# Merge factors loaded ahead of the next pair's inputs, merges and strided items at other steps, in a hybrid decoder step

## The chip, the cores and the metric

The kernel runs on one core of a Trainium2 chip. The core has five engines with a program of their own each: TensorE (PE in the profile; PEld is its loading of weights), VectorE (DVE), ScalarE (ACT), GpSimd (POOL) and SyncE (SP), which in this kernel issues nearly all DMAs. The metric is the device time of one execution in microseconds (us), as the median of several runs.

## The reference

One layer of a decoder on a prompt of 2048 positions (width 1024) and on 32 sample rows (8 sequences of 4 positions, each with a cache of 2048 keys and values). Everything is float32.

```python
q, k, v, u, vg = split(rmsnorm(x) @ w_in)
outs, lses = [], []
for (w, d), bias in zip(((128, 1), (512, 4), (2048, 16)), biases):   # 8 heads of 64
    o, lse = dilated_attention(q, k, v, bias, d, w // d + 1)
    outs.append(o); lses.append(lse)
weights = softmax(stack(lses), axis=0)
att = sum(weights[..., None] * stack(outs))                            # the merge
gate = spatial_gate(layernorm(vg))
x = x + concat([att, u * gate]) @ w_out
x = x + swiglu(rmsnorm(x))
y = rmsnorm(x)
```

Outputs are y for prompt and samples, and the new windows of keys and values.

## The kernel before

The work has three parts in time: the input projection (with the attention of the sample rows beside it), the attention of the prompt, and the output projection with the feed-forward block. The change concerns the middle part and its two borders.

**Order.** The whole order is written out by hand. A `Plan` (L46) collects calls as (step, phase) and then emits them sorted by step, and within a step by ten phases: early, exp, low, scores, turn, mid, values, out, misc, store. Every engine and SP executes its own instructions in the order in which they were emitted. An instruction that waits holds everything behind it on its engine; for SP this means that a DMA that can't be issued yet holds all later DMAs. A step is a place in this order and no length of time.

**Pairs and items.** The 8 heads are worked in 4 pairs, `p` = 0 to 3. Prompt attention begins at step B0 = 240; a pair has 20 units of two steps, so a stage of NI = 40 steps. L = 399 is the step where the pairs end. Sixteen units of a pair are band items (numbered 0 to 15, 128 queries each; branches 1 and 2 together), four are strided items ("s", the third branch). The lists FIRST, OTHER and LAST (L1137 to L1139) give the order of units for pair 0, for pairs 1 and 2, and for pair 3. A unit with index i of its pair has its scores at step X = stage start + 2i + 1.

- A band item: scores on PE (`pair_scores`, L890 and L897), bias and row minimum on DVE (L903), exponential on ACT (L908), transposes on PE (L919), values on PE (L942, L952), output to `ob` by ACT (L959).
- A strided item: `strided_order` (L967, two copies on POOL at X-4) gathers its keys and queries into `sq`; scores on PE at X (L977); bias and minimum on DVE for each head of the pair (L984, L985, at X+1 and X+2); a subtraction on POOL (L989, at X+2 and X+3); exponential on ACT (L992); row sums on DVE (L996); transposes on PE (L1001, at X+5 and X+6), copied by ACT (L1003); values on PE (L1010); output to `o3` by ACT (L1017).

**Merging.** When a pair is through, `Stats` turns minima and sums into the two merge factors per position and head: a selection on POOL (L1034), a small matmul (L1040), arithmetic on DVE (L1050 to L1066), and a store to `f_d` in DRAM by eight DMAs (L1073), at step 6 of the next pair's stage. `merge_load(p, j)` (L1079, DMAs at L1087) loads the factors for two blocks of 256 positions, j and j+1, spread over the partitions, two DMAs of 256 KB into one "pair" tile of which there are two. `merge` (L1091) needs three POOL instructions for each of the eight blocks: L1096 (`ob` times factor), L1098 (`o3` times factor), L1100 (sum). `merge_store` (L1102) writes the merged rows to `cat_d`, four blocks at a time. All this is planned beside the work of the next pair; only the output projection reads `cat_d`.

For pair 3 the first four blocks are merged before L: blocks 0 and 2 by DVE, 1 and 3 by POOL (L1183). The other four are merged in the output projection.

**Other loads in these stages.** `load_head(p)` (L851) loads the next pair's q and k (1 MB each, L857), bias (L860), values in the strided order (L845) and values in band order (four DMAs with short rows, L849), planned at steps 4, 6, 8, 15 and 18 of the stage before (L1166). `load_far` (L878) loads the values of branch 2's far keys. `sgu_sample_cat_load` (L1110, DMA at L1112) loads the 32 sample rows' attention and gate output from `cs_d` into a "pair" tile at step B0+19; `sgu_sample_cat` (L1114) transposes them on PE at step B0+22 (L1119). They were written to `cs_d` before B0 (L617).

**The border to the output projection.** From step L-12 on, weights of w_out are loaded (`load_wo`, L1354) and split into a high and a low part on ACT and POOL (L142, L145); from L-9 on, `early_cat` (L1393) loads rows of `cat_d`, partly into tiles that hold `ob` and `o3` in the pairs.

Of the kernel before, what the change touches and what calls it, by code (L numbers as in the profile page):

```python
# [10 lines left out]
F32 = mybir.dt.float32  # L11
# [8 lines left out]
P = 128  # L20
T = 2048
NT = T // P
# [19 lines left out]
def dap(t, offset, pattern):  # L42
    return bass.AP(tensor=t.tensor, offset=t.offset + offset, ap=pattern)


class Plan:  # L46
# [8 lines left out]
    def at(self, step, phase, fn, *args):  # L55
        self.events.append((step, self.PHASES.index(phase), self.n, fn, args))
        self.n += 1
# [10 lines left out]
def hymba_step(ctx: ExitStack, tc: tile.TileContext, A: dict, O: dict):  # L68
    nc = tc.nc
    sync, act, dve, pool, pe = nc.sync, nc.scalar, nc.vector, nc.gpsimd, nc.tensor  # L70
# [97 lines left out]
    at = plan.at  # L168
# [4 lines left out]
    def zn_tile():  # L173
        return rp.tile([P, 512], F32, name="zn", tag="zn", bufs=3)

    def pair_tile(dtype=F32R):
        return rp.tile([P, 2, 512], dtype, name="pair", tag="pair", bufs=2)
# [4 lines left out]
    def raw_tile():  # L182
        return rp.tile([P, 512], F32, name="raw", tag="raw", bufs=RAW)
# [475 lines left out]
    B0 = 240  # L659
# [22 lines left out]
    for j in range(8):  # L682
        s0 = 105 + 4 * j if j < 3 else 117 + 3 * (j - 3) if j < 6 else 127 + 3 * (j - 6)
# [27 lines left out]
    for half in range(2):  # L711
        for ki, kind in enumerate(ORDER[half]):
            for gi, tiles in enumerate(GROUPS):
# [13 lines left out]
                for j, tj in enumerate(tiles):  # L727
# [24 lines left out]
                    else:  # L752
                        layer_norm(e + 1, t, lambda t=t: zn["g", t], P, lambda t=t: gate_tile(t))

                        f = e + 4 + ((3 if half else 5) if tj in (4, 5) else 0)
# [19 lines left out]
    for n in range(MADE):  # L775
        s0 = 138 + 15 * n
# [11 lines left out]
    for run in key_runs:  # L788
        for j, (b, t, u) in enumerate(run):
            s0 = 36 + i if i < 8 * EARLY else 60 + int((i - 8 * EARLY) * 4 / 3)  # L790
# [12 lines left out]
    for bg in range(2):  # L803
        s0 = (136, V0 + 24)[bg]
# [4 lines left out]
    for b in range(SB):  # L809
        s0 = V0 + 8 * b  # L810
# [266 lines left out]
    mf = {}  # L1077

    def merge_load(p, j):  # L1079

        if p < HP - 1:
            f = pair_tile(F32)
            t_ = f[:, 0], f[:, 1]
        else:
            t_ = raw_tile(), zn_tile()
        for c in range(2):
            sync.dma_start(t_[c], dap(f_d, (p * 8 + j + c) * 2 * CP * 512, [[512, 2 * CP], [0, C // CP], [1, 512]]))  # L1087
            v = t_[c].rearrange("p (i z r) -> p i z r", z=2, r=NT)
            mf[p, j + c] = v[:, :, 0], v[:, :, 1]
# [45 lines left out]
        (strided_scores if its[0]["kind"] == "s" else pair_scores)(*its)  # L1135

    FIRST = [0, 1, 2, 3, "s", 4, 5, "s", 6, 7, 8, "s", 9, 10, 11, "s", 12, 13, 14, 15]  # L1137
    OTHER = [0, "s", 1, 2, 3, 4, "s", 5, 6, 7, 8, "s", 9, 10, 11, 12, "s", 13, 14, 15]
    LAST = ["s", 0, 1, "s", 2, 3, "s", 4, 5, "s", 6, 7] + list(range(8, NT))  # L1139
    units, taken = [], set()  # L1140
    for p in range(HP):
        r4 = 0
        for n in FIRST if p == 0 else LAST if p == HP - 1 else OTHER:
            X = B0 + 2 * len(units) + 1
# [7 lines left out]
            if n % 2:  # L1152
                grp["y"] = (4, 5, 6) if p == HP - 1 and n == NT - 1 else (6, 6, 7)
                taken.update(range(X + grp["y"][0], X + grp["y"][2]))
    NI = 2 * len(OTHER)
    L = B0 + 2 * len(units) - 1
# [6 lines left out]
    for p in range(1, HP):  # L1163
        s0 = B0 + (p - 1) * NI
        at(s0 + 4, "misc", begin, p)
        for y in (4, 6, 8, 15, 18):  # L1166
            at(s0 + y, "misc", load, p)

    def stats_of(p, steps, r0, r1):
        d = {}  # L1170
        at(*steps[0], lambda: d.update(s=Stats(p, sts[p], r0, r1, dve if r0 else pool)))
        for (y, ph), fn in zip(steps, "a b c weights_e weights_b store".split()):
            at(y, ph, lambda fn=fn: getattr(d["s"], fn)())

    for p in range(HP):
        s0 = B0 + (p + 1) * NI
        if p == HP - 1:
            x = s0 - NI
            stats_of(p, [(x + y, ph) for y, ph in ((26, "early"), (27, "turn"), (28, "early"), (28, "early"), (29, "early"), (29, "mid"))], 0, 64)
            steps = ((2, "early"), (2, "turn"), (3, "early"), (4, "early"), (5, "early"), (5, "early"))  # L1180
            for j in (0, 2):
                at(x + 30, "mid", merge_load, p, j)
            for j, y, eng in ((0, 33, dve), (1, 33, pool), (2, 36, dve), (3, 36, pool)):  # L1183
                for part in range(3):
                    at(x + y + part, "store", merge, p, j, eng, part)
            at(x + 36, "store", merge_store, p, 0, 2)
            at(x + 39, "store", merge_store, p, 2, 4)
        else:
            steps = ((2, "misc"), (3, "misc"), (4, "early"), (5, "early"), (5, "misc"), (6, "mid"))
            fast = p == HP - 2  # L1190
            y0 = 12
            when = [y0 + (i * 2 // 3 if fast else i) for i in range(24)]
            for j in range(0, 8, 2):
                at(s0 + max(8, when[3 * j] - 4) + (j == 2), "mid", merge_load, p, j)
            for i, y in enumerate(when):
                at(s0 + y, "store", merge, p, i // 3, pool, i % 3)
            for j in (0, 4):
                at(s0 + when[3 * j + 11] + 1, "store", merge_store, p, j, j + 4)
        stats_of(p, [(s0 + y, ph) for y, ph in steps], 64 if p == HP - 1 else 0, P)
    for X, its in units:  # L1200
        p, n = its[0]["p"], its[0]["n"]
# [21 lines left out]
        if n % 2:  # L1223
            y = its[0]["grp"]["y"]
# [9 lines left out]
    for n in range(3):  # L1234
        at(B0 + 40 + 30 * n, "store", down_plain, n)

    at(B0 + 19, "misc", sgu_sample_cat_load)
    at(B0 + 22, "scores", sgu_sample_cat)

    plan.run(B0)  # L1240
# [4 lines left out]
    ap_ = left.enter_context(tc.tile_pool(name="attn", bufs=2, reuse_waits="tile"))  # L1245
# [929 lines left out]
    def first_block(B):  # L2175
# [5 lines left out]
        load_cat(B, 0, KD - 1, KD)  # L2181
        load_cat(B, 5, 0, KD)
        merge_load(h, 4)
        merge_load(h, 6)
        load_acc(B, 1)
# [325 lines left out]
```

## Time and profile before

| | us |
|---|---|
| median of 3 runs | 2467.8 (2467.05 to 2472.98) |
| profiled execution, its own time | 2461.96 |
| its span, first to last instruction | 2460.2 |
| PE busy | 2350.1 |
| POOL busy | 1438.1 |
| stretch of pair 0 / 1 / 2 / 3 | 68.7 / 74.2 / 73.5 / 77.9 |
| from the end of the pairs to the end | 1604.4 |

The times of steps below come from the profiled execution, which was 5.8 us faster than the median run. In the profile L12 is line 12 of the kernel, "out<-in" are the names of tiles, and "x4" counts instructions of a kind that were merged into one row. SPq is SP's queue: its durations are the time that SP needed to issue a DMA, not the time of the transfer. A bracket `[6.53 <-ACT e L992]` gives the time for which the engine stood idle before the instruction, and the instruction that released it.

### The profile page before, as it was taken

The numbers are of one execution on the slowest core, as the hardware profiler recorded it, in microseconds if no ns is written. First come the engines' busy times: TensorE is split into PE (matmuls) and PEld (weight loads), VectorE is DVE, ScalarE is ACT, GpSimd is POOL, SyncE is SP. The second block draws the span as 40 slices with busy tenths as digits, with TensorE's granted clock in tenths as the row PEclk, the third lists the DMA queues.
The fourth block names the chain that finished last, engine by engine and source line by source line (L and its number), as shares of the span: only waits on it lengthen the run. The fifth ranks groups of instructions, "written<-read, shape, count | busy, mean of one in ns | idle before, by whom it ended". The sixth has DMA issues, their size and how long they took to land. (4 is left out here: it accounts for less than half of the span.)

```text
span 2460.2 us, 41718 instructions
## 1 busy us (share of the span) xinstructions
PE 2350.1 (96%) x14592; PEld 2026.5 (82%) x14592; DVE 1482.7 (60%) x2902; ACT 1203.3 (49%) x2745; POOL 1438.1 (58%) x1153
## 2 busy tenths in 40 slices
PE   8999999997988899999999999999999998999998
PEld 6877786665666678999999988999999977999997
DVE  3467573114555534767777676566666666677676
ACT  6424333224555546656665546444443446555555
POOL 2225463112345646888788764756666563888885
PEclk9999999998989898999999999999999998999999
DMA  9864856786554564887877654766666644878552
GB/s 276 248 193 138 247 160 212 226 255 172 143 149 119 153 199 137 256 265 229 256 243 232 209 164 152 262 205 215 200 214 216 212 125 164 271 244 249 172 171 88
DMA packets 333365, 494.61 MB, mean 201 GB/s; under 512 B 42903, under 2 KB 174176, under 8 KB 329572
## 3 DMA queue, kind: packets, MB, share of 16 engines
q1 hardware_dynamic: 326308, 479.90, 63.4%
q10 hardware_dynamic: 6848, 12.06, 1.8%
q8 instruction: 115, 1.88, 0.3%
q14 instruction: 94, 0.77, 0.1%
HBM read 404.72 MB, written 168.98 MB: 233 GB/s over the span
## 5 line engine op out<-in xcount | busy, mean ns | idle before, releaser
L1626 POOL TENSOR_TENSOR op<-fr,op 128x512 fp32r<-128x512 f32 x392 | 522.5, 1342 | 350.6 <-ACT op L1622 262.1
L1863 PE MATMUL ps_m<-xh,op 128*128 128x384 f32 (+3 forms) x1344 | 429.9, 320 | 3.9 <-DVE raw L1874 3.5
L1864 PE MATMUL ps_m<-xl,op 128*128 128x384 f32 (+3 forms) x1344 | 428.6, 319 | 1.6 <-POOL xl L145 1.5
L1865 PE MATMUL ps_m<-xh,op 128*128 128x384 f32 (+3 forms) x1344 | 429.0, 319 | 0.0
L1716 DVE TENSOR_TENSOR acc<-acc,ps_o 128x512 f32<-128x512 f32 x448 | 300.3, 684 | 71.1 <-PE ps_o L1714 63.8
L1714 PE MATMUL ps_o<-hop 128*128 128x512 f32 x1142 | 322.6, 394 | 1.7 <-DVE hop L1695 1.0
L1863 PEld LDWEIGHTS ps_m<-xh,op 128*128 128x128 f32 x1344 | 256.7, 191 | 13.2 <-DVE raw L1874 6.7
L1864 PEld LDWEIGHTS ps_m<-xl,op 128*128 128x128 f32 x1344 | 256.4, 191 | 7.3 <-POOL xl L145 2.0
L1865 PEld LDWEIGHTS ps_m<-xh,op 128*128 128x128 f32 x1344 | 256.3, 191 | 0.0
L1714 PEld LDWEIGHTS ps_o<-hop 128*128 128x128 f32 x1142 | 209.4, 188 | 37.7 <-DVE hop L1695 2.8
L1622 ACT ACTIVATE op<-fr 128x512 fp32r<-128x512 f32 x396 | 239.3, 621 | 0.0
L325 PE MATMUL ps_s<-wh,xh 128*128 128x512 f32 x480 | 197.1, 411 | 6.1 <-ACT xh L142 6.0
L326 PE MATMUL ps_s<-wl,xh 128*128 128x512 f32 x480 | 190.0, 396 | 0.0
L327 PE MATMUL ps_s<-wh,xl 128*128 128x512 f32 x480 | 189.7, 395 | 0.0
L1863 PE MATMUL ps_t<-xh,op 128*128 128x384 f32 (+2 forms) x560 | 180.7, 323 | 5.5 <-ACT xh L1512 2.5
L1864 PE MATMUL ps_t<-xl,op 128*128 128x384 f32 (+2 forms) x560 | 179.9, 321 | 0.5 <-DVE xl L1534 0.3
L1865 PE MATMUL ps_t<-xh,op 128*128 128x384 f32 (+2 forms) x560 | 179.9, 321 | 0.0
L546 POOL TENSOR_TENSOR pr<-kv,qb 96x512 f32<-96x512 f32 x32 | 46.5, 1452 | 158.1 <-DMA kv<-in_cache_k_dram 77.0
L1695 POOL TENSOR_TENSOR hop<-hop 128x512 fp32r<-128x512 f32 x96 | 130.9, 1364 | 11.9 <-ACT hop L1691 11.4
L325 PEld LDWEIGHTS ps_s<-wh,xh 128*128 128x128 f32 x480 | 91.6, 191 | 41.4 <-issue 16.8
L1714 PE MATMUL ps_m<-hop 128*128 128x512 f32 x384 | 119.5, 392 | 0.0
L1877 ACT ACTIVATE zn<-zn 128x384 f32<-128x384 f32 (+2 forms) x65 | 31.6, 487 | 171.5 <-DVE zn L1876 171.5
(568 smaller groups left out, 5391.3 us busy)
## 6 DMA issues: line engine op xcount, KB each, us to landing
fr<-ab_d SPq DMA_DIRECT2D x308, 256.0 KB
hop<-dd_d SPq DMA_DIRECT2D x143, 256.0 KB
out_ks_dram<-in_cache_k_dram SPq DMA_DIRECT2D x56, 512.0 KB
out_vs_dram<-in_cache_v_dram SPq DMA_DIRECT2D x56, 512.0 KB
ab_d<-fr SPq DMA_DIRECT2D x88, 256.0 KB
dwx<-dd_d SPq DMA_DIRECT2D x71, 256.0 KB
ab_d<-pair SPq DMA_DIRECT2D x63, 256.0 KB
kv<-in_cache_k_dram SPq DMA_DIRECT2D x64, 192.0 KB
```

Of the source, the lines that this page charges most:

```text
L325: pe.matmul(o[j], xh[:, k, :], wh, start=(k == 0), stop=False)
L326: pe.matmul(o[j], xh[:, k, :], wl, start=False, stop=False)
L327: pe.matmul(o[j], xl[:, k, :], wh, start=False, stop=(k == KD - 1))
L546: eng.tensor_mul(pr[0:n], x[0:n], q[0:n])
L1622: act.activation(ops[f, j][0], ab[f][j], AF.Copy)
L1626: (pool if f > 1 or j in POOL_LOW[f] or B.b0 else dve).tensor_sub(lo_, ab[f][j], hi.bitcast(F32))
L1695: (pool if B.b0 or k >= 7 * (NF // 2 - 1) else dve).tensor_sub(lo_, lo_.bitcast(F32), hi.bitcast(F32))
L1714: pe.matmul(ps, l_, r_, start=(new and y == 0), stop=(y == 2), skip_group_check=True)
L1716: dve.tensor_add(x[:, cs], x[:, cs], ps)
L1863: pe.matmul(out, wh[:, ks], xh[:, :, k], start=(k == 0 and q not in (2, 4, 6)), stop=False, skip_group_check=True)
L1864: pe.matmul(out, wh[:, ks], xl[:, :, k], start=False, stop=False, skip_group_check=True)
L1865: pe.matmul(out, wl[:, ks], xh[:, :, k], start=False, stop=(k == 3), skip_group_check=True)
```

## The change

With s0 the start of the stage in which a pair's merge is done:

- `merge_load` takes its tiles for j = 4 and 6 from two new buffers "mf" (4 KB per partition each); for j = 0 and 2 it uses the two "pair" tiles as before.
- The four calls of `merge_load` stand at s0+7 to s0+10. They stood at s0+8, 15, 20 and 26 (for the merge of pair 2: 8, 13, 16 and 20).
- Merges begin at s0+15 (for the merge of pair 2 at s0+14); they began at s0+12. Their stores move with them.
- q, k and bias of pairs 2 and 3 are loaded at steps 11, 12 and 13 of the stage before, not at 4, 6 and 8. Pair 1's are left.
- In OTHER the four strided items have places 3, 8, 12 and 16 of 20 instead of 1, 6, 11 and 16; in LAST 2, 4, 7 and 9 instead of 0, 3, 6 and 9.
- In pair 3, block 2 is merged by POOL instead of DVE, blocks 2 and 3 at other steps, and each has a store of its own.
- The sample rows are loaded at B0+2 instead of B0+19.

```diff
     def merge_load(p, j):
         if p < HP - 1:
-            f = pair_tile(F32)
+            f = pair_tile(F32) if j < 4 else ap_.tile([P, 2, 512], F32, name="mf", tag="mf", bufs=2)
...
-    OTHER = [0, "s", 1, 2, 3, 4, "s", 5, 6, 7, 8, "s", 9, 10, 11, 12, "s", 13, 14, 15]
-    LAST = ["s", 0, 1, "s", 2, 3, "s", 4, 5, "s", 6, 7] + list(range(8, NT))
+    OTHER = [0, 1, 2, "s", 3, 4, 5, 6, "s", 7, 8, 9, "s", 10, 11, 12, "s", 13, 14, 15]
+    LAST = [0, 1, "s", 2, "s", 3, 4, "s", 5, "s", 6, 7] + list(range(8, NT))
...
         at(s0 + 4, "misc", begin, p)
-        for y in (4, 6, 8, 15, 18):
+        for y in (11, 12, 13, 15, 18) if p > 1 else (4, 6, 8, 15, 18):
             at(s0 + y, "misc", load, p)
...
-            for j, y, eng in ((0, 33, dve), (1, 33, pool), (2, 36, dve), (3, 36, pool)):
+            for j, y, eng in ((0, 33, dve), (1, 33, pool), (2, 35, pool), (3, 38, pool)):
                 for part in range(3):
                     at(x + y + part, "store", merge, p, j, eng, part)
             at(x + 36, "store", merge_store, p, 0, 2)
-            at(x + 39, "store", merge_store, p, 2, 4)
+            at(x + 39, "store", merge_store, p, 2, 3)
+            at(x + 42, "store", merge_store, p, 3, 4)
...
-            y0 = 12
+            y0 = 14 if fast else 15
             when = [y0 + (i * 2 // 3 if fast else i) for i in range(24)]
             for j in range(0, 8, 2):
-                at(s0 + max(8, when[3 * j] - 4) + (j == 2), "mid", merge_load, p, j)
+                at(s0 + 7 + j // 2, "mid", merge_load, p, j)
...
-    at(B0 + 19, "misc", sgu_sample_cat_load)
+    at(B0 + 2, "misc", sgu_sample_cat_load)
```

## The prediction

> **What bounds the kernel now.** I read the page first, for the engine that sets the span.
>
> ```profile
> PE 2350.1 (96%) x14592; PEld 2026.5 (82%) x14592; DVE 1482.7 (60%) x2902; ACT 1203.3 (49%) x2745; POOL 1438.1 (58%) x1153
> ```
>
> PE is the bound on the whole, so time is won only where PE stands still or runs at a low clock. The busy times by stretch say where. I cut at the first score matmul of each of the four head pairs (561.5, 630.2, 704.4, 777.9) and at the first matmul of the output projection (855.8). The columns are the stretch, its length, then the busy time of PE, PEld, DVE, ACT and POOL, PE's granted clock, the DMA share and GB/s.
>
> ```profile
> 561.50:630.20 68.70, 54.07 (x763) 40.17 (x762) 34.89 (x98) 36.52 (x102) 16.75 (x16) 0.88 0.61 165
> 630.20:704.40 74.20, 61.95 (x866) 45.78 (x864) 40.96 (x118) 38.75 (x111) 36.73 (x41) 0.89 0.62 156
> 704.40:777.90 73.50, 62.18 (x863) 45.99 (x862) 39.60 (x113) 38.53 (x109) 36.69 (x41) 0.88 0.59 152
> 777.90:855.80 77.90, 67.79 (x921) 49.40 (x920) 44.74 (x130) 45.70 (x125) 50.41 (x54) 0.89 0.46 132
> 855.80:2460.20 1604.40, 1562.82 (x8654) 1431.97 (x8650) 1063.54 (x1963) 838.09 (x1964) 1120.72 (x872) 0.98 0.65 205
> ```
>
> Behind 855.8 PE is busy for 1562.8 of 1604.4 us, so what the pairs save should reach the end. In the pairs it idles 10 to 15 us each and has only 0.88 to 0.89 of its clock. No other engine is near full there, so these are waits in a chain, not a full engine. PE's timeline gives each wait: start, duration, instruction, and in brackets the idle time before it and its releaser.
>
> ```profile
> 600.30 1.03 PE L1119 MATMUL ps_t<-ident,pair 32*128 32x32 f32 x8 [11.16 <-DMA pair<-cs_d]
> 643.23 0.70 PE L890 MATMUL ps_s<-k,q 64*128 64x256 f32 x4 [1.83 <-DVE st L903]
> 659.53 0.66 PE L1001 MATMUL ps_t<-ident,e 128*128 128x128 f32 x4 [2.39 <-ACT e L992]
> 682.31 1.11 PE L1001 MATMUL ps_t<-ident,e 128*128 128x128 f32 x4 [6.53 <-ACT e L992]
> 717.50 0.70 PE L890 MATMUL ps_s<-k,q 64*128 64x256 f32 x4 [1.83 <-DVE st L903]
> 733.19 1.12 PE L1001 MATMUL ps_o<-ident,e 128*128 128x128 f32 x4 [1.50 <-ACT e L992]
> 756.27 1.12 PE L1001 MATMUL ps_t<-ident,e 128*128 128x128 f32 x4 [6.16 <-ACT e L992]
> 809.14 0.66 PE L1001 MATMUL ps_o<-ident,e 128*128 128x128 f32 x4 [1.31 <-ACT e L992]
> 839.64 1.22 PE L890 MATMUL ps_s<-k,q 64*128 64x256 f32 x4 [3.10 <-DVE st L903]
> ```
>
> The transposes of line 1001 wait for ACT's exponential of a strided item, and that waits for POOL's subtraction (L989). POOL's own timeline shows what holds it:
>
> ```profile
> 655.32 0.73 POOL L1096 TENSOR_TENSOR ob<-ob,pair 128x256 f32<-128x256 f32 x1 [12.08 <-DMA pair<-f_d]
> 679.88 0.72 POOL L1096 TENSOR_TENSOR ob<-ob,pair 128x256 f32<-128x256 f32 x1 [6.60 <-DMA pair<-f_d]
> 680.56 1.04 POOL L989 TENSOR_TENSOR e<-e,st 128x512 f32<-128x512 f32 x1
> ```
>
> POOL works in program order: it stands 6.60 us in a merge that lacks its factors, and the subtraction that PE needs is next in its queue. SP's timeline shows why the factors, and the sample rows, are late:
>
> ```profile
> 552.57 0.56 SPq L617 DMA_DIRECT2D cs_d<-po_d  x1
> 574.66 15.58 SPq L849 DMA_DIRECT2D v<-v_d  x4
> 590.28 4.72 SPq L1112 DMA_DIRECT2D pair<-cs_d  x1
> 642.36 5.04 SPq L1073 DMA_DIRECT2D f_d<-f  x8
> 653.28 15.31 SPq L849 DMA_DIRECT2D ve<-v_d  x4
> 668.69 3.54 SPq L1087 DMA_DIRECT2D pair<-f_d  x2
> ```
>
> The four gathering loads of the next pair's values (L849) hold SP for 15.58 and 15.31 us. The sample rows' load (L1112) and the factors for j=4 (L1087 at 668.69) stand behind them; the latter also need a "pair" buffer that earlier merges still read.
>
> The last view is PE's clock in the stretch after each wait (columns as above):
>
> ```profile
> 600.30:604.50 4.20, 4.20 (x36) 3.81 (x38) 0.42 (x1) 1.60 (x5) 0.00 (x0) 0.50 0.01 4
> 604.50:610.00 5.50, 5.50 (x82) 4.29 (x80) 3.31 (x6) 1.50 (x4) 1.05 (x2) 0.83 0.00 0
> 643.20:647.70 4.50, 4.47 (x44) 3.47 (x44) 3.17 (x11) 3.08 (x11) 0.04 (x1) 0.62 0.18 29
> 659.50:664.50 5.00, 4.87 (x38) 3.09 (x38) 2.98 (x8) 3.97 (x12) 2.73 (x3) 0.66 1.06 226
> 682.30:687.00 4.70, 4.69 (x34) 3.43 (x34) 2.25 (x6) 3.56 (x11) 4.70 (x7) 0.50 0.54 167
> 717.50:722.20 4.70, 4.70 (x46) 3.46 (x46) 3.14 (x11) 2.99 (x11) 0.00 (x0) 0.65 0.16 24
> 733.10:738.20 5.10, 5.01 (x34) 3.44 (x34) 2.26 (x6) 4.05 (x13) 2.76 (x4) 0.50 1.05 223
> 756.20:761.50 5.30, 4.96 (x38) 3.31 (x40) 3.00 (x8) 4.11 (x13) 5.30 (x7) 0.65 0.55 180
> ```
>
> After each wait PE is busy for some 5 us at 0.50 to 0.66 of its clock. I price that as length times the missing share; a wait costs itself and this.
>
> **The change part by part.** *A, sample rows' load from step B0+19 to B0+2.* The same one DMA is now asked for ahead of the pair 0 and pair 1 loads, SP's 15.58 us among them, at about 565 (561.5 and two steps of 68.7/40 us). What it reads was asked for at 552.57, and its buffer is idle by then. That the write has landed follows from the quiet DMA engines (share 0.00):
>
> ```profile
> 556.00:559.00 3.00, 3.00 (x15) 2.49 (x14) 0.00 (x0) 0.00 (x0) 0.00 (x0) 1.00 0.00 0
> ```
>
> So SP does not stop, and the load has over 20 us until PE asks for it, at 589. The loads that it passes lose one small issue, at nothing: they are for later items, and if that cover failed it would cost PE as long as the load takes. Gain: 11.16 + 4.20 x 0.50 + 5.50 x 0.17 = 14.2 us.
>
> *B, the two long waits.* All eight factor loads of a stage are now asked for in steps 7 to 10, straight behind the store of the factors (642.36 + 5.04 in this stage) and ahead of q, k, bias and values of the next pair. Those move to steps 11 to 18 for pairs 2 and 3. They have the rest of a 40-step stage to land and are no longer in front of anything urgent, so I cost their delay at nothing; it would show as a wait at the next pair's first scores. With two "mf" buffers no factor load waits for a merge. Gain: 6.53 + 4.70 x 0.50 = 8.9, and 6.16 + 5.30 x 0.35 = 8.0; sum 16.9.
>
> *C, the two short ones*, at the first merge of each stage: the loads land sooner (no 1 MB load of k in front), the merge begins at step 15 instead of 12, and the next subtraction stands at step 19, no longer between the first merges. Gain: 2.39 + 5.00 x 0.34 = 4.1, and 1.50 + 5.10 x 0.50 = 4.05; sum 8.1. What is late next on POOL? Its durations:
>
> ```profile
> L1098 POOL TENSOR_TENSOR o<-o,pair x24: 859/892/912, 656.0 to 823.9; 128x256 f32<-128x256 f32 x24
> L967 POOL COPY sq<-k x15: 1068/1109/1161, 570.8 to 804.5; 128x512 f32<-128x512 f32 x15
> ```
>
> Between the subtractions at steps 20 and 27 lie seven merge instructions (at most 0.9 each) and two copies (1.1 each): 8.5 us. A step lasts 74.2/40 = 1.86 us now, about 1.45 with the waits gone, so seven steps are 10 us. POOL keeps up, by a margin of 1.5 us.
>
> *D, strided items two units later in OTHER.* The waits of 1.83 are for DVE, in whose first steps the softmax weights and the first strided item fell together. One DVE instruction of that item:
>
> ```profile
> 638.00 0.69 DVE L985 TENSOR_REDUCE st<-e 128x4 f32<-128x512 f32 x1
> ```
>
> The item has six over the same 512 columns, so some 4.1 us (an estimate) leave the steps ahead of that wait. At most this wins 1.83 + 4.50 x 0.38 = 3.5 and 1.83 + 4.70 x 0.35 = 3.5, sum 7.0; at least nothing, if the work collides a few steps on. I take 4: each of the two waits is shorter than the work that goes.
>
> *E, pair 3's items and merges.* Its factor loads too stop waiting for buffers. The 1.31 us wait can go; the 3.10 us one comes from DVE's own merge of j=0, which stays. In LAST a copy still falls between two subtractions. Between 0 and 5 us (1.31, a clock share like C's, a little of the 3.10): I take 1.5.
>
> *F, the tail.* Three merge instructions go from DVE to POOL, queued between weight splits (L145); pair 2's last merge store moves from step L-11 to L-9. There it stands behind pair 3's first factor loads and directly ahead of the loads of output-projection inputs that reuse its buffer, so SP must now wait for it to land, and the weight loads with it:
>
> ```profile
> 837.75 4.67 SPq L1354 DMA_DIRECT2D v<-in_w_out_dram  x2
> 846.59 0.63 ACT L142 ACTIVATE op<-v 128x512 fp32r<-128x512 f32 x1 [5.79 <-DMA v<-in_w_out_dram]
> 847.30 1.27 POOL L145 TENSOR_TENSOR op<-v,op 128x512 fp32r<-128x512 f32 x1 [5.16 <-ACT op L142]
> ```
>
> The three instructions (at most 2.7 us) fit in POOL's 5.16 us and cost nothing. But SP already spends 4.67 us on these weights, and ACT stands 5.79 us for them, with pair 3's last exponentials behind it. Up to 6 us lost, if a landing of up to 5 us (as long as the wait on SP here) goes straight to PE with some clock; nothing if it fits in SP's wait. I take 4 lost, nearer the upper end, since ACT already waits for just these loads.
>
> *G, new short waits*, at the moved items: bounds 0 and 6 (four like the 1.50). I take 2 lost.
>
> Sum: 14.2 + 16.9 + 8.1 + 4 + 1.5 - 4 - 2 = 38.7 us. The profiled execution took 2461.96 us (span 2460.2); less 38.7 is 2423.3. The median of the three runs is 2467.8, 5.8 above it, so the forecast is **2429 us**. About 0.3% (7.4 us) is what a measurement of this kernel can tell from no change.
>
> **A rule against the rows.** After the waits of 1.50 and 1.83 us PE ran for 5 us at 0.50 to 0.65. The Trainium skill, page "TensorE: Matmul & The Clock Gate", section "HAM oscillation — how this bites in real kernels", gives the rule as no PE-idle gaps over about 3.4 us. By it only the three long waits would cost clock. The rows differ from it, and I go by the rows; what it would give is the third rival.
>
> **The rivals.**
> *Only the long waits go.* POOL's order and DVE's load shift the short waits instead of ending them, so C, D and E bring nothing: 14.2 + 16.9 - 6 = 25 us, 2443. For it: a margin of 1.5 us on POOL is thin. Against: the short waits too were for a load.
>
> *The factors are still late.* SP waits in order for their store, and the loads in a queue that L849 fills; then only A and D come, less F: 14 us, 2454. For it: POOL waited 12.08 us for the first ones. Against: nothing large is now between store and load.
>
> *Short waits cost no clock.* Then C is 2.39 + 1.50 = 3.9 and D half: 6 us less, 2435. Against: the clock rows.
>
> *Slower: POOL becomes the bound.* Merges now end at step 38. If POOL ran late at each of the 12 strided items of pairs 1 to 3, each would cost PE its lateness and the clock. The 1.50 us wait cost 4.05. Twelve of these are 49 us, more than all gains (44.7 before F and G): 2467.8 - 44.7 + 4 + 49 = 2476. It decides from 1.5 us of lateness at every item. Against: POOL is busy 36.7 of 74 us, and would be 36.7 of some 58.
>
> **How the numbers follow.** Forecast 0.66, only the long waits 0.16, factors late 0.08, no clock cost 0.05, POOL bound 0.03; 0.02 for no change from causes that I don't see. The first four are all faster by over 0.3%: 0.95; same 0.02; slower 0.03. The range goes down to 2416 (A to E at their ends, 14.2 + 16.9 + 8.1 + 7 + 5 = 51) and up to 2447, past the second case; the factors-late case and the last two stay out, 0.13 with the tails a little more.
>
> **What would show it.** Right: the sample transposes (L1119) without a wait; the eight factor loads in one run on SP ahead of q; no POOL idle time in L1096 that a subtraction stands behind; PE's waits at L1001 under 1 us, its clock in pairs 0 to 2 near 0.95, and those stretches near 55, 60 and 60 us; the time behind the first output-projection matmul unchanged at 1604 us. Wrong: a wait of PE for q, k or v at the start of a pair; POOL without idle time and PE's waits at L1001 all still there; or the last stretch longer by what the pairs won.

## The result, and the profile after

The changed kernel takes 2429.55 us (median of 4 runs, 2425.58 to 2430.74) beside 2469.82 us for the kernel before, measured beside it (2467.05 to 2472.98): a ratio of 0.9834, 95% interval 0.9815 to 0.9852. That is 40.3 us less, where 38.7 were forecast; the forecast of 2429 us and its range hold. Its profiled execution took 2430.68 us with a span of 2428.9. Behind the one line that the diff adds (L1188) its line numbers are one higher than before: L1416 is now L1417.

The page's first line, as before:

```profile
PE 2338.1 (96%) x14592; PEld 2015.1 (83%) x14592; DVE 1478.2 (61%) x2899; ACT 1202.1 (49%) x2745; POOL 1441.6 (59%) x1156
```

PE has lost 12.0 us of busy time with the same 14592 matmuls, at a mean granted clock of 0.982 instead of 0.974. The busy times by stretch, cut at the pairs' first score matmuls and the first output-projection matmul (columns as in the prediction):

```profile
563.70:618.50 54.80, 51.36 (x763) 37.74 (x762) 34.81 (x98) 36.40 (x102) 14.64 (x14) 0.97 0.75 208
618.50:679.70 61.20, 56.97 (x864) 42.13 (x862) 39.48 (x118) 38.68 (x111) 36.78 (x41) 1.00 0.72 173
679.70:740.00 60.30, 57.08 (x864) 42.03 (x862) 38.12 (x113) 38.52 (x109) 38.96 (x43) 1.00 0.73 183
740.00:818.70 78.70, 65.55 (x921) 48.51 (x920) 44.31 (x128) 45.69 (x125) 52.75 (x56) 0.88 0.48 143
818.70:2428.90 1610.20, 1563.76 (x8652) 1430.49 (x8648) 1064.51 (x1962) 837.81 (x1964) 1122.04 (x874) 0.98 0.65 205
```

Read against the prediction's first windows: pairs 0, 1 and 2 are 13.9, 13.0 and 13.2 us shorter, with the clock up from 0.88 and 0.89 to 0.97 and 1.00. Pair 3 is 0.8 us longer, and what follows is 5.8 us longer. So the gain was made in the first three pairs, and something was paid at the end of the fourth.

PE's timeline after: of the nine waits shown before, those at L1119 and L1001 and the two of 1.83 us are gone. In pairs 0 to 2 most of what remains is short (first line below). Two waits there are longer: 1.87 us for values in pair 0 (L1010, 2.02 before) and 1.34 us in pair 1 (L897), for which the profile shows no releaser. Then come the three large ones at the end of pair 3:

```profile
637.47 1.09 PE L1010 MATMUL ps_o<-eT,v 128*64 128x128 f32 x14 [0.71 <-ACT eT L1003]
797.42 1.22 PE L890 MATMUL ps_s<-k,q 64*128 64x256 f32 x4 [4.12 <-DVE st L903]
810.36 1.85 PE L919 MATMUL ps_t<-ident,e 128*128 128x128 f32 x6 [5.76 <-ACT e L908]
813.42 0.90 PE L919 MATMUL ps_o<-ident,e 128*128 128x128 f32 x3 [1.22 <-ACT e L908]
```

The wait of 5.76 us is new. SP's timeline has both stories:

```profile
565.65 0.62 SPq L1112 DMA_DIRECT2D pair<-cs_d  x1
576.77 14.96 SPq L849 DMA_DIRECT2D v<-v_d  x4
627.05 5.02 SPq L1073 DMA_DIRECT2D f_d<-f  x8
633.32 2.55 SPq L1087 DMA_DIRECT2D pair<-f_d  x4
636.41 2.85 SPq L1087 DMA_DIRECT2D mf<-f_d  x4
639.37 0.78 SPq L857 DMA_DIRECT2D q<-qk_d  x1
649.08 16.63 SPq L849 DMA_DIRECT2D ve<-v_d  x4
794.50 0.46 SPq L1104 DMA_DIRECT2D cat_d<-ob  x1
802.01 0.99 SPq L1394 DMA_DIRECT2D cr<-cat_d  x2
803.04 1.03 SPq L1355 DMA_DIRECT2D v<-in_w_out_dram  x2
```

The sample rows are asked for 11 us ahead of the gathering loads that held them, and all eight factor loads between the store and q, 10 us ahead of L849, which still holds SP for 16.63 us but nothing urgent any more. At the end of pair 3 SP stands from 794.96 to 802.01 behind its own store (L1104): the rows' load (L1394) reuses the store's tile, and by the kernel it also reads rows of `cat_d` that this store writes. Either way it can't go before the store has landed, and the output weights (L1355) are queued behind it. ACT then waits for these weights, with pair 3's last exponentials behind it:

```profile
809.10 0.63 ACT L142 ACTIVATE op<-v 128x512 fp32r<-128x512 f32 x1 [10.52 <-DMA v<-in_w_out_dram]
```

10.52 us instead of 5.79. POOL's waits for factors, from the view of waits in pairs 1 and 2 (us in total, times, longest), before:

```profile
POOL ob L1096 <- DMA pair<-f_d: 44.8, 6, 12.1
```

and after:

```profile
POOL e L989 <- DVE st L985: 27.0, 6, 7.7
POOL ob L1096 <- DMA pair<-f_d: 3.4, 3, 1.3
POOL e L989 <- PE ps_o L952: 2.6, 2, 1.5
```

No row for "mf" appears: those factors were always there in time.

### The profile page after: what moved, and what is told of

It reads as the page before. It is cut to its first block, busy times and chain, and to the rows that moved or that the text cites. A ratio compares the mean times of both kernels' runs of the same rounds, so it can differ in the third digit from the quotient of the medians.

```text
span 2428.9 us, 41733 instructions
## 1 busy us (share of the span) xinstructions
PE 2338.1 (96%) x14592; PEld 2015.1 (83%) x14592; DVE 1478.2 (61%) x2899; ACT 1202.1 (49%) x2745; POOL 1441.6 (59%) x1156
## 5 line engine op out<-in xcount | busy, mean ns | idle before, releaser
L1864 PEld LDWEIGHTS ps_m<-xh,op 128*128 128x128 f32 x1344 | 253.8, 189 | 13.1 <-DVE raw L1875 6.3
L1866 PEld LDWEIGHTS ps_m<-xh,op 128*128 128x128 f32 x1344 | 253.3, 188 | 0.0
L1864 PEld LDWEIGHTS ps_t<-xh,op 128*128 128x128 f32 x560 | 106.9, 191 | 13.1 <-DVE raw L1875 3.0
```

What stands on the lines that cost most here:

```text
L1864: pe.matmul(out, wh[:, ks], xh[:, :, k], start=(k == 0 and q not in (2, 4, 6)), stop=False, skip_group_check=True)
L1866: pe.matmul(out, wl[:, ks], xh[:, :, k], start=False, stop=(k == 3), skip_group_check=True)
```

## The experiments

Each is compared with the kernel before, measured beside it on the same chip. The median of the kernel before differs from one such comparison to the next (2465.49 to 2469.82), so ratios are compared, and times only where both kernels were measured together. "Stretch" is the length between the cuts used above, from the profile.

**The sample rows alone.** The kernel before with

```diff
-    at(B0 + 19, "misc", sgu_sample_cat_load)
+    at(B0 + 2, "misc", sgu_sample_cat_load)
```

> The kernel before with one edit: the sample rows are loaded at step B0+2. If the wait was only SP's order, the 11.16 us wait of PE at L1119 and the slow clock behind it go: 14 us less than before (about 0.57%), and the stretches of pairs 1 to 3 stay at 74, 74 and 78 us with all their waits. If another wait takes its place (the loads of pair 0's values, pushed back, or the strided item behind it), less than 7 us.

Measured: ratio 0.9943 (0.9923 to 0.9963), 2453.46 beside 2466.59 us, 13 us less. By stretch:

```profile
564.20:619.30 55.10, 51.47 (x763) 37.58 (x762) 34.81 (x98) 36.58 (x103) 16.75 (x16) 0.97 0.75 205
619.30:691.70 72.40, 61.67 (x865) 45.70 (x864) 40.97 (x118) 38.62 (x110) 36.71 (x41) 0.91 0.62 161
691.70:764.40 72.70, 62.43 (x865) 46.47 (x864) 39.61 (x113) 38.53 (x109) 36.73 (x41) 0.88 0.61 154
```

Pair 0 is 13.6 us shorter (68.7 to 55.1); pairs 1 and 2 are what they were within 2 us. Nothing took the wait's place.

**The loads alone.** The kernel before with the "mf" buffers, the factor loads at `s0 + 7 + j // 2` and pairs 2 and 3's q, k and bias at 11, 12 and 13; no other edit.

> The kernel before with only the loads moved: factor loads at steps 7 to 10 with the two added buffers, q, k and bias of pairs 2 and 3 behind them. Merges, items and the sample rows stay. If the long waits came from the loads' place in SP's queue, the waits of PE at L1001 (6.53, 6.16, 2.39, 1.50) go, those of 1.83 at L890 stay, and the kernel takes 17 to 27 us less than before. If the steps of merges and items make the gain, the waits at L1001 shift and less than 10 us are won.

Measured: ratio 0.9907 (0.9886 to 0.9928), 23 us less than before. Stretches of pairs 1 and 2:

```profile
634.30:698.70 64.40, 58.64 (x863) 42.78 (x862) 40.87 (x118) 38.65 (x110) 36.72 (x41) 0.97 0.65 174
698.70:763.00 64.30, 58.76 (x863) 43.31 (x862) 39.43 (x113) 38.38 (x109) 36.74 (x41) 0.97 0.66 164
```

and PE's waits in these two pairs:

```profile
PE ps_s L890 <- DVE st L903: 3.7, 2, 1.8
PE ps_t L1001 <- ACT e L992: 0.4, 1, 0.4
```

The two pairs are 9.8 and 9.2 us shorter. The waits at L1001, long and short, are down to 0.4 us with merges and items where they were; the two of 1.8 us at L890 stay. The theory of the steps falls for L1001: the loads did it. Their place and the two added buffers were changed together here; neither was run alone.

**The old items.** The changed kernel with the lists OTHER and LAST of before, measured twice.

> The changed kernel with the two old lists of items, all else changed. If the items' places only end the two waits of 1.83 us and their clock, this is 4 to 8 us slower than the changed kernel and the waits at L890 are back at 1.8 us in pairs 1 and 2. If the places are what lets POOL keep up, the waits at L1001 come back too and it is more than 15 us slower.

> The changed kernel with the old lists of items, again. The traces give 6.7 us for the lists, the runs gave 11 across two calls; if the traces are right, 4 to 8 us more than the changed kernel here.

Measured: ratios 0.9878 (0.9855 to 0.9900) and 0.9879 (0.9862 to 0.9895). The second time it stood beside the changed kernel and took 2434.14 us where that took 2427.01: 7.1 us more. (The first ratio beside the changed kernel's 0.9834 would give 11.) The waits at L890 are back, in pair 1 for instance:

```profile
631.39 0.70 PE L890 MATMUL ps_s<-k,q 64*128 64x256 f32 x4 [1.83 <-DVE st L903]
```

Stretches of pairs 1 and 2 in the second measurement, old items:

```profile
618.40:681.60 63.20, 58.62 (x863) 43.42 (x862) 40.77 (x118) 38.37 (x111) 36.70 (x41) 0.97 0.65 170
681.60:745.90 64.30, 59.45 (x863) 43.73 (x862) 39.40 (x113) 38.49 (x109) 36.70 (x41) 0.95 0.68 172
```

and the changed kernel:

```profile
620.70:682.80 62.10, 58.35 (x863) 43.40 (x862) 39.24 (x117) 38.89 (x111) 36.82 (x41) 0.97 0.72 175
682.80:743.10 60.30, 57.09 (x866) 42.10 (x864) 38.33 (x115) 38.54 (x109) 38.98 (x43) 1.00 0.72 178
```

The lists are worth 1.1 and 4.0 us here, and 2.5 in pair 3 (81.0 and 78.5). The 1.1 understates it: in this execution of the changed kernel PE stood 1.52 us at L897 in pair 1, for no reason that the profile shows, with 5 us at 0.66 of the clock behind it. The waits at L1001 did not come back, so the items' places are not what lets POOL keep up.

**Merges sooner.** The changed kernel with

```diff
-            y0 = 14 if fast else 15
+            y0 = 14 if fast else 12
```

> The changed kernel with merges of pairs 0 and 1 from step 12 again, not 15; loads and items stay as changed. If the loads' place alone took the waits at L1001 away, those stay under 1 us and the stretches of pairs 1 and 2 grow by no more than 1 us each from 61.2 and 60.2. If POOL needs the three steps (a subtraction falls between the first merges while their factors still travel), waits of 1 to 3 us at L1001 come back with their slow clock, 3 to 10 us in all.

Measured: ratio 0.9826 (0.9805 to 0.9848). Pairs 1 and 2:

```profile
619.70:679.80 60.10, 57.11 (x865) 42.22 (x864) 39.47 (x118) 38.58 (x110) 36.78 (x41) 1.00 0.71 176
679.80:740.00 60.20, 56.98 (x865) 42.01 (x864) 38.11 (x113) 38.51 (x109) 38.98 (x43) 1.00 0.74 187
```

60.1 and 60.2 beside 61.2 and 60.3: with the factors there in time, the step at which the merges of pairs 0 and 1 begin makes no difference. "Merges later" has no part in their gain; for pair 2's merge (step 14 instead of 12) it wasn't run.

**The tail: rows' loads behind the weights.** The changed kernel with

```diff
-    for i, y in ((1, -9), (2, -9), (3, -8), (4, -5)):
+    for i, y in ((1, -5), (2, -5), (3, -5), (4, -5)):
```

> The changed kernel with the early loads of attention rows for tiles 1 to 3 planned at step L-5 instead of L-9 and L-8, behind the second four weight loads. If SP's wait of 7.0 us for pair 2's last merge store holds the weights back and ACT and PE with them, the wait of 5.76 us at L919 shrinks to under 2 us with the slow clock behind it, and this is 6 to 9 us faster than the changed kernel. If the weights are late for their own transfer, the wait stays and the time is the same.

Measured: ratio 0.9831 (0.9809 to 0.9853), the same as the changed kernel's. The wait at L919 went, but not the cost. SP:

```profile
795.50 0.46 SPq L1104 DMA_DIRECT2D cat_d<-ob  x1
803.00 3.64 SPq L1394 DMA_DIRECT2D cr<-cat_d  x4
806.68 1.51 SPq L1381 DMA_DIRECT2D pair<-cat_d  x1
```

and PE:

```profile
815.66 0.79 PE L1417 MATMUL ps_m<-op,pair 128*128 128x512 f32 x1 [4.50 <-ACT pair L1408]
```

SP waits 7.0 us for the store here too, with 1 MB of factor loads issued just ahead of it. The weights now go out before that wait, but tile 0's own rows (L1381) still stand behind it, as in the changed kernel, and PE, no longer held at L919, stands for them instead; the 11.3 us behind run at 0.57 of the clock. Neither theory was quite right: SP's wait did hold the weights, but freeing them alone only let the next load behind that wait come last.

**The tail: the store first.** The changed kernel with pair 2's second store in the step of its last merge, which puts it ahead of the factor loads; measured twice.

```diff
-                at(s0 + when[3 * j + 11] + 1, "store", merge_store, p, j, j + 4)
+                at(s0 + when[3 * j + 11] + (0 if fast and j else 1), "store", merge_store, p, j, j + 4)
```

> The changed kernel with pair 2's second merge store one step sooner (L-10), right behind its last merge and so ahead of pair 3's factor loads. If SP's 7.0 us wait for this store is what holds the output weights back, that wait goes, PE's 5.76 us wait at L919 falls to under 2 us as before the change and the pairs' stretch shrinks by 4 to 7 us from 255; DVE's wait for the factors may grow by up to 2 us, since 512 KB now go ahead of them. If the store only moves the wait to another DMA, the stretch stays within 2 us of 255.

> The kernel with pair 2's second merge store one step sooner, again. If the store's place in SP's order costs what the traces of the pairs and of the first output products show, 6 to 9 us less than the changed kernel; if the first measurement was chance, the same within 3 us.

Measured: ratios 0.9797 (0.9775 to 0.9819) and 0.9832 (0.9819 to 0.9845); the second time 2423.37 us beside 2427.01 for the changed kernel, 3.6 us less. SP, first measurement:

```profile
784.57 0.40 SPq L1104 DMA_DIRECT2D cat_d<-ob  x1
789.15 0.98 SPq L1394 DMA_DIRECT2D cr<-cat_d  x2
```

ACT:

```profile
799.94 0.63 ACT L142 ACTIVATE op<-v 128x512 fp32r<-128x512 f32 x1 [7.05 <-DMA v<-in_w_out_dram]
```

PE's wait at L919, 5.76 us in the changed kernel, is 1.06 us here (2.34 in the second measurement):

```profile
801.20 1.85 PE L919 MATMUL ps_t<-ident,e 128*128 128x128 f32 x6 [1.06 <-ACT e L908]
```

Pair 3's stretch and the 11.3 us behind it, second measurement:

```profile
735.30:810.20 74.90, 64.84 (x922) 47.79 (x921) 42.77 (x126) 45.61 (x125) 51.65 (x56) 0.91 0.55 150
810.20:821.50 11.30, 11.19 (x90) 8.75 (x89) 6.95 (x21) 4.59 (x11) 2.23 (x2) 1.00 0.16 42
```

and the same of the changed kernel beside it:

```profile
743.10:821.60 78.50, 65.07 (x921) 48.02 (x920) 44.33 (x128) 45.64 (x125) 52.56 (x56) 0.87 0.49 145
821.60:832.90 11.30, 11.30 (x78) 8.97 (x76) 3.14 (x15) 2.05 (x6) 1.50 (x2) 0.67 0.11 28
```

SP no longer stands 7.0 us for the store. Pair 3 is 3.6 us shorter, and the first output products run at 1.00 of the clock instead of 0.67, worth 11.3 x 0.33 = 3.7 us: 7.3 by the trace, 3.6 by the runs beside it, some 9 by the first ratio beside the changed kernel's 0.9834. The traces and both ratios have the same sign; the size stays open between 3.6 and 9.

**The tail: block 0 later, and all together.** The store first, and pair 3's block 0 merged at x+36; then that with the rows' loads at L-3.

```diff
-            for j, y, eng in ((0, 33, dve), (1, 33, pool), (2, 35, pool), (3, 38, pool)):
+            for j, y, eng in ((0, 36, dve), (1, 33, pool), (2, 35, pool), (3, 38, pool)):
...
-            at(x + 36, "store", merge_store, p, 0, 2)
+            at(x + 39, "store", merge_store, p, 0, 2)
```

> As the last, and pair 3's block 0 merged by DVE three steps later (L-3 instead of L-6). If PE's 4.12 us wait at L890 is only DVE standing in order behind block 0's factors, it goes, and this is 3 to 6 us faster than the last kernel. If the factors are that late for all, the wait moves on to the next scores and nothing is won.

> The sixth kernel, and the early loads of attention rows at step L-3, behind tile 0's own rows. If these loads (1.8 MB) stand in front of the weights and of tile 0's rows, ACT's waits for both shrink, and this is up to 4 us faster than the sixth; together up to 12 us faster than the changed kernel. If they come too late themselves, PE waits for them at the first output-projection units and it is slower than the sixth.

Measured: ratios 0.9810 (0.9787 to 0.9833) and 0.9799 (0.9773 to 0.9825), no better than the store alone (0.9797 in the same comparison). PE in the first of the two:

```profile
808.08 1.84 PE L919 MATMUL ps_t<-ident,e 128*128 128x128 f32 x6 [8.41 <-ACT e L908]
```

The wait at L890 went and more than all of it came back at L919, where ACT waits for the weights: 8.41 us in place of 4.57 and 1.06. So as long as the weights come that late, DVE's standing behind block 0 costs nothing of its own. The weights bound that stretch.

**Store first, rows' loads at L-3,** block 0 as in the changed kernel, measured beside the changed kernel itself.

> The changed kernel again, beside the next three on one chip. 36 to 44 us less than before, a ratio near 0.984.

> Store one step sooner, and the early loads of attention rows at step L-3, behind the weights and tile 0's rows; block 0 of pair 3 as in the changed kernel. If these loads still delay the weights, 1 to 4 us less than with the store alone; if only the transfers' sum counts there, the same.

Measured: the changed kernel again 0.9845 (0.9831 to 0.9859), 2427.01 us; this one 0.9810 (0.9794 to 0.9825), 2417.05 us, 10 us less, and 6.3 less than with the store alone, where 1 to 4 were expected. ACT's wait for the weights:

```profile
800.59 0.63 ACT L142 ACTIVATE op<-v 128x512 fp32r<-128x512 f32 x1 [3.21 <-DMA v<-in_w_out_dram]
```

Pair 3 and what follows it:

```profile
738.80:808.80 70.00, 63.91 (x922) 48.03 (x921) 43.33 (x126) 45.37 (x124) 51.39 (x56) 0.93 0.51 149
808.80:820.10 11.30, 10.96 (x88) 8.28 (x87) 6.90 (x20) 4.74 (x12) 2.71 (x2) 1.00 0.27 73
```

Pair 3 takes 70.0 us, 8.5 less than the changed kernel beside it. PE no longer waits at L919; its wait at L890 (4.19 us) is the one long wait that is left. This version beats both kernels, by 10 and 48 us.

## Why the prediction was right, and where not

The theory was that SP's order made the loads late and POOL's and PE's order passed that on. The rival was that the steps of merges and items make the gain. The experiments bear the theory out for the waits; several sizes were off and cancelled each other, so it is in part luck that 38.7 stands so close to 40.3. By steps:

- *A*, forecast 14.2: 13.9 in the changed kernel, 13.6 alone. Right, the clock share included.
- *B and C*, forecast 16.9 and 8.1: the loads alone took 9.8 and 9.2 from pairs 1 and 2, 19.0 in all, and ended short and long waits alike. The mechanism is right; the size is 6 us too large. The waits at L1001 went from 16.6 us to 0.4, but PE's idle time in the two pairs fell by 12.3 only, since other short waits grew (those at L1010 from 1.7 to 4.1), and its busy time fell by 6.7, where the clock shares were put at 8.5. Of C's three reasons only the earlier loads count: with the old merge step and with the old items the waits stayed away.
- *D*, forecast 4: the lists are worth 5.1 us in pairs 1 and 2 by the trace, and 7.1 in all by the runs, pair 3 included.
- *G*, forecast 2 lost: the sum of B, C, D and G was 27.0, and pairs 1 and 2 gained 26.2. That it fits hides two errors: B and C brought 6 us less than forecast, and all else in these pairs 7.2 instead of 2, of which the lists are 5.1 and the rest isn't attributed. POOL's margin of 1.5 us held: before the subtractions at step 27 it stood 1.51 and 1.13 us (the row L989 <- PE above), and even the old merge steps would have done.
- *E*, forecast 1.5, bounds 0 and 5: from pair 3's start to its wait at L890 it took 61.7 us (777.9 to 839.64) and takes 57.4 (740.0 to 797.42), 4.3 less. With the old lists the same way took 60.3 us beside 57.5, so 2.8 of it is the list LAST.
- *F*, forecast 4 lost, bounds 0 and 6: from there to the first output product it took 16.2 us and takes 21.3, 5.1 more; then 11.3 us run at 0.64 of the clock, where PE had 1.00 before:

```profile
818.70:830.00 11.30, 11.30 (x77) 8.80 (x74) 2.88 (x13) 1.69 (x5) 1.32 (x2) 0.64 0.13 33
```

```profile
855.80:867.00 11.20, 11.20 (x95) 9.02 (x92) 6.46 (x20) 4.52 (x10) 0.00 (x0) 1.00 0.13 32
```

That is another 11.3 x 0.36 = 4.1, so 9.2 lost. This is the step that was mis-sized most: "Up to 6 us lost, if a landing of up to 5 us (as long as the wait on SP here) goes straight to PE with some clock". SP stood 7.0 us for the store, with 1 MB queued ahead of it, and the clock stayed low for 11.3 us into the output projection, which the prediction had put at no change. How low varies: in the kernel with merges sooner, whose tail is the same, it was 0.83.

By the trace the terms give 13.9 + 26.2 + 4.3 - 9.2 = 35.2 us where 38.7 were forecast: E brought 2.8 us more and F cost 5.2 more. The two profiled spans differ by only 31.3: the changed one lost 2.2 us ahead of the pairs, where nothing was changed (that part took 560.3 to 567.0 us in the traces of this case), and 1.7 behind. The medians differ by 40.3 in the first comparison and by 38.5 (2465.49 to 2427.01) in the last. The profiled execution of before was 7.9 us faster than the median of the first comparison, that of after 1.1 slower; that is the whole way from 31.3 to 40.3, and why executions of one kernel differ by that much isn't shown. The prediction carried 5.8 us of it over by starting from the median.

*The buffer.* The prediction also says that the factors for j=4 waited for a "pair" buffer that earlier merges still read. Before, POOL's last read of it in pair 0's merge was

```profile
660.45 0.91 POOL L1098 TENSOR_TENSOR o<-o,pair 128x256 f32<-128x256 f32 x1
```

and SP was in L849 until 668.59. So the buffer was free 7.2 us before SP came to that load (4.1 us in the next pair): the place held the two loads behind the long waits, not the buffer. Whether the new place would do without the two added buffers isn't shown.

*Rivals.* "Only the long waits go" fell with the loads alone. "The factors are still late" fell: POOL's wait for them went from 44.8 to 3.4 us. "POOL becomes the bound" fell: its subtractions wait 27.0 us for DVE, and PE's waits at L1001 are 0.2 us each. "Short waits cost no clock" was true in part, below. Of the signs that were named, the idle time in L1096 is left in three places of at most 1.34 us (a subtraction stands behind one of them, of 0.73 us, and waits 5.50 us for DVE afterwards anyway), and one failed: the time behind the first output product grew by 5.8 us, 4.1 of them F's clock.

## What to carry to other kernels

Before moving work, look at what a DMA queue holds in order: a load that nobody needs yet can hold one that everybody needs, and where the engine that waits also carries the next engine's input, the wait is passed on (here to POOL, then ACT, then PE with its clock). When a store is moved, follow it to its landing and count what is already queued ahead of it, who reuses its tile and who reads what it wrote; by the trace the tail gave back 9.2 us, about a fifth of what the others gained (13.9 + 26.2 + 4.3 = 44.4), and the store's place is 3.6 to 9 us of that. An experiment that removes one wait should be read by the whole stretch, since in the tail two waits out of three only moved.

## What the runs showed of the hardware

Equal waits cost PE's clock unequally. The wait of 1.83 or 1.84 us at L890 stands twice in each of five traces (before, the sample rows alone, the loads alone, the old items in both measurements). In eight of the ten places it was followed by 4.5 to 4.7 us at 0.50 to 0.65 of the clock, and in two by full clock, here in the sample rows' kernel:

```profile
632.20:636.90 4.70, 4.20 (x64) 2.86 (x64) 3.22 (x13) 3.79 (x13) 0.09 (x1) 1.00 0.18 28
```

Waits of 0.7 us, as at 637.47 in the changed kernel, left the clock at 1.00. Between them there is no sharp line: the wait of 1.34 us at L897 in the changed kernel was followed by 5 us at 1.00, that of 1.52 us in its second measurement by 5 us at 0.66. The Trainium skill, page "TensorE: Matmul & The Clock Gate", section "Part 1: The HAM clock gate (the "warmup" mystery)", says that activity is watched in windows that run freely; that would let equal waits end differently, though no run here shows the windows. Its figure of about 3.4 us for an idle gap does not hold here: 1.83 us was enough in eight of ten places.

A 512 KB store issued behind 1 MB of loads held SP for 7.0 us; issued ahead of them (the store first), the load that must wait for it went out 4.2 us after it, with the four factor loads issued in between.

Four loads of 256 KB in pieces of 512 bytes (L849) held SP for 15.0 to 16.6 us in the changed kernel's three stages, and with it every DMA behind them; two loads of 1 MB (L857) took it 1.0 to 2.4 us. What in the small pieces costs that time, no run here separates.
